# A two-block transformer on one core: sparse attention with the softmax's division on the output, and a schedule planned with other durations

## The chip, the cores and the metric

One Trainium2 chip, one core. The metric is the time of one execution on the device in microseconds (us); the median over runs is shown. The engines are PE (TensorE matmul; PEld is its weight load), DVE (VectorE), ACT (ScalarE), POOL (GpSimd) and SP (SyncE, which issues the DMAs).

## What is computed

Two layers of a hybrid attention model (latent attention, grouped attention, a depthwise convolution), then a second block with gated linear attention, a sparse attention, a feed-forward network and three layer norms, all over 1024 positions of width 1024. The part that the change rewrites is the sparse attention: 16 heads, 1024 queries, keys and values in one latent of 128, where a query sees the causal keys that an indexer selected (at most 256).

```python
def one_block(args):
    ...
    kv_sel = jax.vmap(lambda c, i: c[i])(ckv, idx)
    logits = jnp.einsum('bqhc,bqkc->bqhk', q_b, kv_sel).astype(jnp.float32) * (dc ** -0.5)
    logits = jnp.where(valid[:, :, None, :], logits, -jnp.inf)
    probs = jax.nn.softmax(logits, axis=-1).astype(kv_sel.dtype)
    return jnp.einsum('bqhk,bqkc->bqhc', probs, kv_sel)
...
o_b = dsa_attention(q_b, c_kv, iq_b, ik, iw_b)
o_b = jnp.einsum('blhc,hcd->blhd', o_b, w_uv[i]).reshape(B, L, DSA_HEADS * DSA_HEAD_DIM)
```

## The kernel before

The program is not written in the order in which it runs. Its text records operations (class `Plan`, calls such as `tt`, `act`, `copy`, `mm`, `tr`, `dma`): each has the tiles that it reads and writes, and in `alts` the engines that may run it with a price for each. Additions and subtractions between SBUF tiles may go to DVE or POOL, copies and casts to ACT or DVE, matmuls only to PE. `Plan.schedule` then plays through the program with these prices: whenever an engine is free in its model, it takes the ready operation that comes first in the text, within a window of 1500 operations. Where several engines could run an operation, it takes the cheapest, unless the wait there (its present work, and 0.6 us for each ready operation) is longer than the dearer price. The result is one fixed order per engine, and the assignment of operations to engines and tiles to slots: 89 pages of 128x512 (`pg`), 8 PSUM banks (`ps`), 8 small buffers (`sm`). On the chip every engine runs its list in order and waits by semaphores. The prices are written by hand, as `(n * 1.04 + 68) / 1000` us for an operation of n columns on DVE (`c_v`), `(n * 2.1 + 150) / 1000` on POOL (`c_p`), and likewise in `c_act`, `copy`, `scale`, `ts`, `mm` and `tr`.

Matrix products are made in three passes: each factor is split into a rounded part and the rest (`split`: a cast or copy and a subtraction), and three matmuls add up in PSUM. All of them are recorded by the same lines: L384 is `mm`, L388 `tr` (a transpose by PE), L325 and L327 are `tt` on DVE and on POOL, L284 is `act`, L293 a copy or cast on DVE, L335 `stt`, L347 `ts`, L358 and L360 `scale` on ACT and on DVE.

The sparse attention (tag `dsa`, from L1738) goes through 8 pairs of heads, 2 heads `i` in each and 2 halves `c` of the queries, 4 query blocks of 128 in each half: 32 units. A unit has three parts: *lead* (the scores of each block by matmuls, the mask's addition with the maximum at L1778, Exp with the sum, reciprocal at L1789, scaling of the probabilities), *loop* (per 128 keys the probabilities are transposed by PE, split and multiplied with the values into one PSUM accumulator), and an end that adds the two halves of the accumulator into `ob`. `pipeline` mixes each unit's lead into the loop of the unit before it. A half `c` = 0 sees one stretch of up to 512 keys (`nb` = 1), `c` = 1 two. Maximum, its scaled negative, sum and reciprocal are columns of a small buffer `sm`, one per query block.

Of the kernel before, what the change touches and what calls it, by code (L numbers as in the profile page):

```python
# [163 lines left out]
class Op:  # L164
    __slots__ = ("alts", "reads", "writes", "emit", "idx", "succ", "npred", "allocs", "table", "bufs", "tag", "pr", "late")
# [7 lines left out]
class Plan:  # L173
# [37 lines left out]
    def op(self, alts, reads, writes, emit, table=None):  # L211
        o = Op()
        o.alts = alts
        o.reads = [x for x in reads if isinstance(x, View)]
        o.writes = [x for x in writes if isinstance(x, View)]
        o.emit = emit
        o.table = table
        o.tag = self.tag
        o.late = self.late
        self.cur.append(o)  # L220
        return o
# [39 lines left out]
    def c_act(self, n, src, extra=0):  # L261
        return (n * 0.833 + (52 if isinstance(src, View) and src.psum else 93) + extra) / 1000
# [34 lines left out]
    def copy(self, out, in_, engs="av"):  # L297
        a = {}
        n = out.n
        if "v" in engs:  # L300
            a["v"] = (n * (1.04 if in_.psum else 0.52) + 68) / 1000
# [7 lines left out]
    def c_v(self, n, ex=0):  # L309
        return (n * 1.04 + 68 + ex) / 1000  # L310

    def c_p(self, n):
        return (n * 2.1 + 150) / 1000
# [26 lines left out]
    def ts(self, out, in0, s1, s2, op0, op1=None, accum=None):  # L340
# [8 lines left out]
        return self.op({"v": (out.n * (1.04 if in0.psum or accum is not None else 0.52) + 130 + (127 if accum is not None else 0)) / 1000},  # L349
                       [in0, s1, s2], [out, accum], emit)  # L350

    def scale(self, out, in_, col):
# [9 lines left out]
        return self.op({"v": (n * (1.04 if in_.psum else 0.52) + 130) / 1000, "a": self.c_act(n, in_, 93)},  # L362
# [17 lines left out]
    def mm(self, out, lhsT, rhs, start, stop, cost=None):  # L380
        n = rhs.n
        c = cost or max(n * 1.676 if rhs.ap.dtype == F32 or n < 256 else n * 0.4219, 60) / 1000
# [3 lines left out]
    def tr(self, out, in_, ident):  # L386
        return self.op({"t": 0.109}, [in_, ident], [out],
# [13 lines left out]
    def schedule(self, window=1500, dwindow=1200, boost=0, queue=0.25, verbose=False):  # L401
# [121 lines left out]
        while len(order) < N:  # L523
            progress = False
            for e in engs:
                while busy[e] <= now + 1e-9:
# [43 lines left out]
                    c = o.alts[e]  # L570
                    pre = None
# [797 lines left out]
BIG = -1.0e30  # L1369
# [65 lines left out]
def block2(N, X, Xd, ped, O, dbg=None):  # L1435
# [303 lines left out]
    for hp in range(8):  # L1739
        ob = {}  # L1740
# [18 lines left out]
        for i in range(2):  # L1759
# [5 lines left out]
            for c in C2:  # L1765
                pn = {}
                for t in range(4 * c, 4 * c + 4):
                    qs = slice((t % 4) * 128, (t % 4) * 128 + 128)
                    sm = P.buf("sm", (128, 4, 4), F32).rearrange("p a b -> p (a b)")
                    nb = 1 if t < 4 else 2  # L1770
                    for b in range(nb):
# [5 lines left out]
                        P.vec((n * 1.04 + 200) / 1000, [s, mk[t, b]], [p, sm[:, b:b + 1]],  # L1777
                              lambda e, p=p, s=s, n=n, m=mk[t, b], a=sm[:, b:b + 1]: nc.vector.tensor_tensor_reduce(  # L1778
                                  out=real(p), in0=real(s[:, 0:n]), in1=real(m), scale=1.0, scalar=BIG, op0=OP.add,
                                  op1=OP.max, accum_out=real(a)))  # L1780
                        pn[t, b] = p
                    if nb == 2:
                        P.tt(sm[:, 0:1], sm[:, 0:1], sm[:, 1:2], "max")
                    P.ts(sm[:, 2:3], sm[:, 0:1], -(128.0 ** -0.5), None, "mult")
                    for b in range(nb):
                        P.act(pn[t, b], pn[t, b], "Exp", bias=sm[:, 2:3], scale=128.0 ** -0.5, accum=sm[:, 4 + b:5 + b])
                    if nb == 2:
                        P.tt(sm[:, 4:5], sm[:, 4:5], sm[:, 5:6], "add")
                    P.vec(0.08, [sm], [sm], lambda e, sm=sm: nc.vector.reciprocal(real(sm[:, 6:7]), real(sm[:, 4:5])))  # L1789
                    for b in range(nb):  # L1790
                        P.scale(pn[t, b], pn[t, b], sm[:, 6:7])
# [22 lines left out]
                G, H = slice(64 * i, 64 * i + 64), slice(64 - 64 * i, 128 - 64 * i)  # L1814
                if i == 0:
                    ob[c] = P.pg()
# [3 lines left out]
                if i == 1:  # L1820
                    obd[hp, c] = P.dram((128, 512))
# [219 lines left out]
```

## Time and profile before

| | |
|---|---|
| median of 3 runs | 4151.16 us (4149.66 to 4156.11) |
| the profiled execution | 4150.0 us |
| its span | 4148.1 us |
| granted TensorE clock, mean | 0.98 |
| PE busy | 3908.4 us, 94% |
| DVE busy | 3306.3 us, 80% |
| ACT busy | 2036.4 us, 49% |
| POOL busy | 1430.2 us, 34% |

The busy time of an engine is the union of its instructions' spans. The slices of a page cut the span into 40 equal parts of some 104 us; each digit is the busy share in tenths. A wait's row names the engine and line that waited, and what released it. The granted clock is a share of 2.4 GHz; the records have two levels, 1.2 and 2.4 GHz.

### The profile page before, as it was taken

What the parts mean: (1) busy time and instruction counts of PE and PEld (TensorE: products, weight loads), DVE (VectorE), ACT (ScalarE), POOL (GpSimd) and SP (SyncE); (2) the same over time, 40 slices, a digit from 0 to 9 for tenths busy, and PEclk for the clock granted to TensorE, in tenths of its full rate; (3) what the DMA queues carried; (4) which work ended last, traced back from release to release, by engine and by line L of the source; (5) the groups of instructions that cost most, each with busy time, mean ns of one, the idle gap of its engine ahead of it and who ended that gap; (6) DMA issues with size and microseconds to landing.
All of it is one profiled execution on the core that took longest, in us unless ns stands there. A gap on an engine that the chain in (4) does not pass through costs nothing. (4 is left out here: it accounts for less than half of the span.)

```text
span 4148.1 us, 54250 instructions
## 1 busy us (share of the span) xinstructions
PE 3908.4 (94%) x18536; PEld 3153.5 (76%) x18536; DVE 3306.3 (80%) x5640; ACT 2036.4 (49%) x3969; POOL 1430.2 (34%) x1257
## 2 busy tenths in 40 slices
PE   7989998989989998999999999999999999999988
PEld 4768766667877776778878878888878788888867
DVE  8995899997896789985999996388886865455588
ACT  5244576774334566763545551366663432222245
POOL 4542455663142344552223441011132411121153
PEclk8999999999999999999999999999999999999998
DMA  7132211123323110042111142100044411111121
GB/s 254 62 117 72 62 54 53 50 70 114 110 83 99 39 34 26 16 133 94 67 44 54 67 142 77 62 31 30 32 144 152 137 51 49 49 41 46 56 82 57
DMA packets 184981, 311.88 MB, mean 75 GB/s; under 512 B 22912, under 2 KB 46208, under 8 KB 184704
## 3 DMA queue, kind: packets, MB, share of 16 engines
q1 hardware_dynamic: 184704, 308.42, 23.0%
q8 instruction: 146, 2.39, 0.2%
q14 instruction: 131, 1.07, 0.1%
HBM read 237.81 MB, written 62.39 MB: 72 GB/s over the span
## 5 line engine op out<-in xcount | busy, mean ns | idle before, releaser
L384 PE MATMUL ps<-pg,pg 128*128 128x512 f32 (+4 forms) x17200 | 3843.6, 380 | 119.1 <-ACT pg L284 43.5
L384 PEld LDWEIGHTS ps<-pg,pg 128*128 128x128 f32 (+2 forms) x17200 | 3009.0, 190 | 798.5 <-ACT pg L284 72.9
L327 POOL TENSOR_TENSOR pg<-pg,pg 128x512 fp32r<-128x512 f32 (+4 forms) x935 | 1355.7, 1462 | 2338.7 <-ACT pg L284 1301.7
L284 ACT ACTIVATE pg<-pg 128x512 fp32r<-128x512 f32 (+9 forms) x1529 | 875.5, 601 | 893.5 <-DVE pg L335 240.6
L325 DVE TENSOR_TENSOR pg<-pg,pg 128x512 fp32r<-128x512 f32 (+8 forms) x1126 | 956.2, 868 | 218.7 <-ACT pg L284 162.6
L284 ACT ACTIVATE pg<-ps 128x512 f32<-128x512 f32 (+9 forms) x1351 | 686.8, 557 | 801.4 <-PE ps L384 597.4
L325 DVE TENSOR_TENSOR pg<-ps,pg 128x128 fp32r<-128x128 f32 (+9 forms) x690 | 381.3, 567 | 209.2 <-PE ps L384 146.3
L335 DVE SCALAR_TENSOR_TENSOR pg<-ux,c,pg 128x512 f32<-128x512 f32 x416 | 348.7, 867 | 9.6 <-ACT pg L284 2.2
L368 DVE TENSOR_REDUCE sm<-ps 128x1 f32<-128x512 f32 (+1 forms) x492 | 326.1, 679 | 9.6 <-PE ps L384 7.0
L293 DVE CAST pg<-pg 128x512 fp32r<-128x512 f32 (+4 forms) x387 | 226.9, 596 | 72.0 <-ACT pg L284 34.0
L284 ACT ACTIVATE pg<-ps,c 128x512 f32<-128x512 f32 (+1 forms) x182 | 127.3, 708 | 250.0 <-PE ps L384 218.5
L335 DVE SCALAR_TENSOR_TENSOR pg<-pg,c,pg 128x512 f32<-128x512 f32 (+3 forms) x242 | 220.1, 946 | 5.5 <-ACT pg L284 5.2
L388 PE MATMUL ps<-c,pg 128*128 128x128 f32 (+1 forms) x796 | 180.2, 274 | 14.3 <-DVE pg L293 5.8
L293 DVE COPY ux<-ps 128x512 f32<-128x512 f32 x83 | 57.3, 690 | 143.3 <-ACT pg L284 133.6
L1523 DVE MAX8 sm<-ux 128x8 f32<-128x384 f32 (+5 forms) x192 | 168.8, 887 | 3.3
L1524 DVE MATCH_REPLACE8 ux<-sm,ux 128x384 f32<-128x384 f32 (+5 forms) x192 | 167.7, 875 | 0.0
L384 PE MATMUL ps<-pg,c 128*128 128x512 f32 (+3 forms) x196 | 85.2, 502 | 74.9 <-DVE pg L325 28.6
L388 PEld LDWEIGHTS ps<-c,pg 128*128 128x128 f32 (+1 forms) x796 | 107.6, 141 | 40.3 <-issue 6.2
L284 ACT ACTIVATE pg<-pg,sm 128x512 f32<-128x512 f32 (+2 forms) x192 | 116.2, 606 | 11.2 <-DVE sm L347 10.7
L384 PEld LDWEIGHTS ps<-pg,c 128*128 128x128 f32 (+2 forms) x196 | 33.6, 176 | 105.7 <-DVE pg L325 31.6
L671 ACT ACT_TABLE_LOAD x84 | 107.8, 1283 | 1.5
L1778 DVE CUSTOM_DVE_ANT_0 pg<-ps,pg 128x512 f32<-128x512 f32 (+3 forms) x176 | 100.0, 575 | 8.5 <-PE ps L384 6.3
(74 smaller groups left out, 1017.2 us busy)
## 6 DMA issues: line engine op xcount, KB each, us to landing
d<-pg SPq DMA_DIRECT2D x202, 256.0 KB, 2.1
pg<-d SPq DMA_DIRECT2D x178, 256.0 KB, 3.3
pg<-in_w2a SPq DMA_DIRECT2D x108, 256.0 KB, 2.8
pg<-in_wmod SPq DMA_DIRECT2D x96, 256.0 KB, 3.1
pg<-in_wup SPq DMA_DIRECT2D x88, 256.0 KB, 2.7
pg<-in_win SPq DMA_DIRECT2D x80, 256.0 KB, 3.3
pg<-in_wout SPq DMA_DIRECT2D x64, 256.0 KB, 3.3
pg<-in_wdn SPq DMA_DIRECT2D x48, 256.0 KB, 2.7
```

Of the source, the lines that this page charges most:

```text
L284: nc.scalar.activation(real(out), real(in_), fn, scale=real(scale), **k)
L293: self.nc.vector.tensor_copy(real(out), real(in_))
L325: self.nc.vector.tensor_tensor(out=real(out), in0=real(in0), in1=real(in1), op=o)
L327: self.nc.gpsimd.tensor_tensor(out=real(out), in0=real(in0), in1=real(in1), op=o)
L335: self.nc.vector.scalar_tensor_tensor(out=real(out), in0=real(in0), scalar=real(scalar), in1=real(in1), op0=o0, op1=o1)
L368: lambda e: self.nc.vector.tensor_reduce(out=real(out), in_=real(in_), axis=AX.X, op=o))
L384: lambda e: self.nc.tensor.matmul(real(out), lhsT=real(lhsT), rhs=real(rhs), start=start, stop=stop))
L388: lambda e: self.nc.tensor.transpose(real(out), real(in_), real(ident)))
L671: nc.scalar.preload_act_table_set(pre)
L1523: P.vec(P.c_v(n), [w], [m8], lambda e, m8=m8, w=w: nc.vector.max(real(m8), real(w)))
L1524: P.vec(P.c_v(n), [w, m8], [w], lambda e, m8=m8, w=w: nc.vector.match_replace(real(w), real(m8), real(w), MARK))
L1778: lambda e, p=p, s=s, n=n, m=mk[t, b], a=sm[:, b:b + 1]: nc.vector.tensor_tensor_reduce(out=real(p), in0=real(s[:, 0:n]), in1=real(m), sca ...
```

## The change

Three things are edited. In the sparse attention the four query blocks of a unit share one small buffer, so that the scaled negative maximum, the sum over the two stretches and the reciprocal are one operation on four columns each; the second stretch's maximum starts from the first's. The probabilities are not scaled any more: the four reciprocals are transposed by PE, spread over 64 partitions, into one PSUM bank, copied to `rr`, and the output `ob` of two heads is multiplied with it once. The prices are others, among them one for transposes that falls from 0.109 to 0.06 us. And an operation on DVE that reads SBUF alone (`dual`) gets dearer in the planner's model while POOL is busy there.

```diff
+        o.dual = "v" in alts and not any(x.psum for x in o.reads) and sum(x.n > 64 for x in o.reads) > 0
...
-        return (n * 0.833 + (52 if isinstance(src, View) and src.psum else 93) + extra) / 1000
+        return (n * 0.836 + (170 if isinstance(src, View) and src.psum else 202) + extra) / 1000
...
-            a["v"] = (n * (1.04 if in_.psum else 0.52) + 68) / 1000
+            a["v"] = (n * (1.04 if in_.psum else 0.52) + 155) / 1000
...
-        return (n * 1.04 + 68 + ex) / 1000
+        return (n * 1.04 + 155 + ex) / 1000
-        return (n * 2.1 + 150) / 1000
+        return (n * 2.2 + 200) / 1000
...
-        return self.op({"v": (out.n * (1.04 if in0.psum or accum is not None else 0.52) + 130 + (127 if accum is not None else 0)) / 1000},
+        return self.op({"v": (out.n * (1.04 if in0.psum or accum is not None else 0.52) + 190 + (127 if accum is not None else 0)) / 1000},
...
-        return self.op({"v": (n * (1.04 if in_.psum else 0.52) + 130) / 1000, "a": self.c_act(n, in_, 93)},
+        return self.op({"v": (n * (1.04 if in_.psum else 0.52) + 190) / 1000, "a": self.c_act(n, in_, 93)},
...
-        c = cost or max(n * 1.676 if rhs.ap.dtype == F32 or n < 256 else n * 0.4219, 60) / 1000
+        c = cost or max(n * 1.774 if rhs.ap.dtype == F32 or n < 256 else n * 0.4434 + 1, 60) / 1000
-        return self.op({"t": 0.109}, [in_, ident], [out],
+        return self.op({"t": 0.06}, [in_, ident], [out],
...
+                    if e == "v" and o.dual and busy["p"] > now:
+                        c += 0.42 * min(busy["p"] - now, c / 0.58)
```

(the planner's prices above; the sparse attention below)

```diff
@@ -1764,31 +1768,33 @@
                 split(*qq[c], o[c])
             for c in C2:
                 pn = {}
+                G, H = slice(64 * i, 64 * i + 64), slice(64 - 64 * i, 128 - 64 * i)
+
+                sm = P.buf("sm", (128, 4, 4), F32)
+                nb = 1 + c
                 for t in range(4 * c, 4 * c + 4):
                     qs = slice((t % 4) * 128, (t % 4) * 128 + 128)
-                    sm = P.buf("sm", (128, 4, 4), F32).rearrange("p a b -> p (a b)")
-                    nb = 1 if t < 4 else 2
+                    top = sm[:, 0, t % 4:t % 4 + 1]
                     for b in range(nb):
                         n = mw(t, b)
                         s = P.ps(max(n, 256))
                         N.mm(s, N.p3((qq[c][0][:, qs], qq[c][1][:, qs]),
                                      (cT[b][0][:, 0:max(n, 256)], cT[b][1][:, 0:max(n, 256)])))
                         p = P.pg()[:, 0:n]
-                        P.vec((n * 1.04 + 200) / 1000, [s, mk[t, b]], [p, sm[:, b:b + 1]],
-                              lambda e, p=p, s=s, n=n, m=mk[t, b], a=sm[:, b:b + 1]: nc.vector.tensor_tensor_reduce(
-                                  out=real(p), in0=real(s[:, 0:n]), in1=real(m), scale=1.0, scalar=BIG, op0=OP.add,
-                                  op1=OP.max, accum_out=real(a)))
+                        first = [top.k(t)] if b else []
+                        P.vec((n * 1.04 + 200) / 1000, [s, mk[t, b]] + first, [p, top.k(t)],
+                              lambda e, p=p, s=s, n=n, m=mk[t, b], a=top, b=b: nc.vector.tensor_tensor_reduce(
+                                  out=real(p), in0=real(s[:, 0:n]), in1=real(m), scale=1.0, scalar=real(a) if b else BIG,
+                                  op0=OP.add, op1=OP.max, accum_out=real(a)))
                         pn[t, b] = p
-                    if nb == 2:
-                        P.tt(sm[:, 0:1], sm[:, 0:1], sm[:, 1:2], "max")
-                    P.ts(sm[:, 2:3], sm[:, 0:1], -(128.0 ** -0.5), None, "mult")
+                P.ts(sm[:, 0, :], sm[:, 0, :], -(128.0 ** -0.5), None, "mult")
+                for t in range(4 * c, 4 * c + 4):
                     for b in range(nb):
-                        P.act(pn[t, b], pn[t, b], "Exp", bias=sm[:, 2:3], scale=128.0 ** -0.5, accum=sm[:, 4 + b:5 + b])
-                    if nb == 2:
-                        P.tt(sm[:, 4:5], sm[:, 4:5], sm[:, 5:6], "add")
-                    P.vec(0.08, [sm], [sm], lambda e, sm=sm: nc.vector.reciprocal(real(sm[:, 6:7]), real(sm[:, 4:5])))
-                    for b in range(nb):
-                        P.scale(pn[t, b], pn[t, b], sm[:, 6:7])
+                        P.act(pn[t, b], pn[t, b], "Exp", bias=sm[:, 0, t % 4:t % 4 + 1].k("e"), scale=128.0 ** -0.5,
+                              accum=sm[:, 1 + b, t % 4:t % 4 + 1].k((t, b)))
+                if nb == 2:
+                    P.tt(sm[:, 1, :], sm[:, 1, :], sm[:, 2, :], "add")
+                P.vec(0.2, [sm], [sm], lambda e, sm=sm: nc.vector.reciprocal(real(sm[:, 3, :]), real(sm[:, 1, :])))
                 lead = P.take(cut)
                 P.side()
                 acc = P.ps()
...
@@ -1811,13 +1817,18 @@
                         P.mm(d, st_, mv, j == 0 and z == 0, j == nj - 1 and z == 1)
                 loop = P.take(cut)
                 P.side()
-                G, H = slice(64 * i, 64 * i + 64), slice(64 - 64 * i, 128 - 64 * i)
+
+                rp = P.ps()
+                for t in range(4):
+                    P.tr(rp[0:64, t * 128:(t + 1) * 128], sm[:, 3, t:t + 1].to_broadcast([128, 64]), ident)
                 if i == 0:
-                    ob[c] = P.pg()
+                    ob[c], rr[c] = P.pg(), P.pg()
+                P.copy(rr[c][G, :].k(i), rp[0:64, :])
                 t = P.pg()
                 P.copy(t[G, :], acc[H, :])
                 P.tt(ob[c][G, :].k(i), acc[G, :], t[G, :], "add")
                 if i == 1:
+                    P.tt(ob[c], ob[c], rr[c], "mult", "vp")
                     obd[hp, c] = P.dram((128, 512))
                     P.dma(obd[hp, c], ob[c])
                 units.append([lead, loop, P.take(cut)])
```

The prices move instructions in the whole program. In total PE has 128 rows more, all of them transposes of `sm`; DVE has 5342 rows before and 4606 now, ACT 3747 and 3759 with every repetition counted, POOL 1262 and 1531. Three places:

POOL at the program's beginning, before. Subtractions `a<-b,c` are the rests of split weights; `pg_213` is a running sum of seven squares for the first norm.

```order
L327 TENSOR_TENSOR pg_136<-pg_94,pg_128 128x256
L327 TENSOR_TENSOR pg_158<-pg_104,pg_148 128x256
L327 TENSOR_TENSOR pg_213<-pg_213,pg_260 128x512
L327 TENSOR_TENSOR pg_314<-pg_221,pg_301 128x512
L327 TENSOR_TENSOR pg_333<-pg_227,pg_323 128x512
L327 TENSOR_TENSOR pg_365<-pg_249,pg_348 128x512
L327 TENSOR_TENSOR pg_385<-pg_262,pg_376 128x512
```

And now:

```order
L329 TENSOR_TENSOR pg_134<-pg_92,pg_122 128x512
L329 TENSOR_TENSOR pg_159<-pg_100,pg_138 128x256
L329 TENSOR_TENSOR pg_174<-pg_106,pg_154 128x256
L329 TENSOR_TENSOR pg_190<-pg_116,pg_171 128x256
L329 TENSOR_TENSOR pg_220<-pg_220,pg_227 128x512
L329 TENSOR_TENSOR pg_220<-pg_220,pg_249 128x512
L329 TENSOR_TENSOR pg_220<-pg_220,pg_266 128x512
```

POOL took one of the seven additions to the running sum before; now (`pg_220`) it takes four, three of them in a row, and the first split of a 128x512 weight.

PE in the first unit of the sparse attention, before: transposes of probabilities (L388, `c_82` is the identity, `ps_26610` and `ps_26621` are PSUM banks) among matmuls of the query projection (`ps_26495`, `ps_26597`).

```order
L388 MATMUL ps_26610<-c_82,pg_26529 128x128
L388 MATMUL ps_26621<-c_82,pg_26529 128x128
L384 MATMUL ps_26495<-pg_19133,pg_26322 128x512
L384 MATMUL ps_26597<-pg_19473,pg_26322 128x512
L384 MATMUL ps_26495<-pg_19145,pg_26322 128x512
L384 MATMUL ps_26597<-pg_19491,pg_26322 128x512
L384 MATMUL ps_26495<-pg_19133,pg_26329 128x512
L388 MATMUL ps_26610<-c_82,pg_26537 128x128
L388 MATMUL ps_26621<-c_82,pg_26537 128x128
L388 MATMUL ps_26610<-c_82,pg_26549 128x128
```

And now, at the end of that unit's transposes (`ps_26637` is the bank for the reciprocals, `sm_26532` their buffer):

```order
L390 MATMUL ps_26611<-c_82,pg_26549 128x128
L390 MATMUL ps_26617<-c_82,pg_26549 128x128
L390 MATMUL ps_26625<-c_82,pg_26549 128x128
L390 MATMUL ps_26635<-c_82,pg_26549 128x128
L390 MATMUL ps_26637<-c_82,sm_26532 64x128
L386 MATMUL ps_26505<-pg_19185,pg_26325 128x512
L390 MATMUL ps_26637<-c_82,sm_26532 64x128
L386 MATMUL ps_26505<-pg_19164,pg_26332 128x512
L390 MATMUL ps_26637<-c_82,sm_26532 64x128
L390 MATMUL ps_26647<-c_82,pg_26556 128x128
L390 MATMUL ps_26637<-c_82,sm_26532 64x128
L386 MATMUL ps_26505<-pg_19177,pg_26325 128x512
```

The four new transposes stand singly between projection matmuls and transposes of probabilities.

DVE inside the sparse attention, before: merges, scalings of the maximum and reciprocals of single query blocks, and a scaling of probabilities (L360).

```order
L1789 RECIPROCAL sm_28597<-sm_28597 128x1
L325 TENSOR_TENSOR sm_28622<-sm_28622 128x1
L325 TENSOR_TENSOR pg_28669<-ps_28644,pg_28669 128x4x64
L360 TENSOR_SCALAR pg_28613<-pg_28613,sm_28597 128x128
L347 TENSOR_SCALAR sm_28622<-sm_28622 128x1
L325 TENSOR_TENSOR sm_28658<-sm_28658 128x1
L325 TENSOR_TENSOR sm_28689<-sm_28689 128x1
L325 TENSOR_TENSOR pg_28727<-ps_28683,pg_28727 128x4x64
L347 TENSOR_SCALAR sm_28658<-sm_28658 128x1
L347 TENSOR_SCALAR sm_28689<-sm_28689 128x1
L325 TENSOR_TENSOR pg_28767<-pg_28681,pg_28754 128x512
```

And now, the same kinds of operation for one unit:

```order
L349 TENSOR_SCALAR sm_28472<-sm_28472 128x4
L327 TENSOR_TENSOR pg_28549<-ps_28519,pg_28549 128x4x64
L295 COPY pg_28612<-ps_28569 64x512
L327 TENSOR_TENSOR pg_28625<-ps_28569,pg_28612 64x512
L295 CAST pg_28642<-ps_28533 128x512
L327 TENSOR_TENSOR pg_28653<-ps_28533,pg_28642 128x512
L295 CAST pg_28662<-ps_28638 128x4x64
L295 CAST pg_28668<-ps_28614 128x512
L327 TENSOR_TENSOR sm_28472<-sm_28472 128x4
L327 TENSOR_TENSOR pg_28682<-ps_28614,pg_28668 128x512
L327 TENSOR_TENSOR pg_28691<-ps_28616,pg_28672 128x512
L1797 RECIPROCAL sm_28472<-sm_28472 128x4
```

One scaling, one merge and one reciprocal of 128x4 serve four blocks, and splits of probabilities (casts and subtractions) stand between them.

## Rows read from the trace of the kernel before

**Rows 1.** Page, parts 1 and 2: busy times; PE's and DVE's forty slices.

```profile
PE 3908.4 (94%) x18536; PEld 3153.5 (76%) x18536; DVE 3306.3 (80%) x5640; ACT 2036.4 (49%) x3969; POOL 1430.2 (34%) x1257
...
PE   7989998989989998999999999999999999999988
...
DVE  8995899997896789985999996388886865455588
```

**Rows 2.** Busy time by stretch: PE, PEld, DVE, ACT, POOL (instructions), granted clock, DMA.

```profile
0.00:300.00 300.00, 249.28 (x1151) 190.49 (x1152) 285.41 (x392) 128.15 (x236) 153.26 (x99) 0.93 0.44 146
...
500.00:900.00 400.00, 356.51 (x1584) 270.47 (x1584) 384.69 (x589) 283.24 (x551) 244.59 (x212) 0.96 0.17 50
...
1400.00:1800.00 400.00, 369.74 (x1579) 277.64 (x1578) 367.25 (x570) 268.56 (x497) 209.60 (x201) 0.98 0.12 35
...
2000.00:2500.00 500.00, 476.30 (x2634) 409.59 (x2633) 481.12 (x867) 266.56 (x572) 180.58 (x154) 0.99 0.23 79
...
2700.00:3000.00 300.00, 298.54 (x1658) 246.50 (x1657) 250.82 (x839) 201.75 (x517) 38.71 (x71) 1.00 0.10 31
...
3900.00:4100.00 200.00, 180.08 (x838) 147.18 (x837) 169.00 (x203) 88.92 (x145) 85.97 (x59) 0.95 0.21 63
...
4100.00:4148.00 48.00, 30.35 (x215) 28.70 (x214) 37.73 (x77) 24.78 (x53) 18.93 (x22) 0.80 0.21 68
```

**Rows 3.** Waits of PE in the whole span: total us, times, longest us.

```profile
PE ps L384 <- ACT pg L284: 52.5, 37, 8.7
PE ps L384 <- DVE pg L325: 47.0, 43, 8.2
...
PE ps L384 <- POOL pg L327: 28.7, 29, 5.9
```

**Rows 4.** Waits of PE from 2660 to 3090 us, the sparse attention.

```profile
PE ps L384 <- DVE pg L293: 2.0, 1, 2.0
PE ps L388 <- ACT pg L358: 1.6, 2, 1.3
PE ps L388 <- DVE pg L360: 1.4, 3, 0.8
```

**Rows 5.** Groups by line and form: operations of the sparse attention's softmax.

```profile
L284 ACT ACTIVATE pg<-pg,sm 128x512 f32<-128x512 f32 x96 | 68.4, 713 | 3.2 <-DVE sm L347 2.8
...
L284 ACT ACTIVATION_READ_ACCUMULATOR pg<-pg,sm 128x1 f32 x192 | 36.3, 189 | 0.0
...
L360 DVE TENSOR_SCALAR pg<-pg,sm 128x512 f32<-128x512 f32 x52 | 25.5, 492 | 1.0
...
L325 DVE TENSOR_TENSOR sm<-sm 128x1 f32<-128x1 f32 x128 | 25.0, 208 | 5.6 <-ACT pg L284 5.4
```

**Rows 6.** Timeline of PE in the sparse attention: start us, us, line, operation, count.

```profile
2864.05 0.27 PE L388 MATMUL ps<-c,pg 128*128 128x128 f32 x1
...
2866.03 0.60 PE L388 MATMUL ps<-c,pg 128*128 128x128 f32 x4
2866.38 4.83 PE L384 MATMUL ps<-pg,pg 128*128 128x512 f32 x20
```

**Rows 7.** Timeline of DVE and POOL: start us, us, line, operation, count.

```profile
702.00 1.82 DVE L325 TENSOR_TENSOR pg<-pg,pg 128x512 fp32r<-128x512 f32 x1
...
702.00 1.28 POOL L327 TENSOR_TENSOR pg<-pg,pg 128x512 fp32r<-128x512 f32 x1 [1.07 <-ACT pg L284]
...
2647.92 0.69 DVE L325 TENSOR_TENSOR pg<-pg,pg 128x512 fp32r<-128x512 f32 x1 [0.76 <-ACT pg L284]
...
3399.60 0.42 DVE L293 CAST pg<-pg 128x512 fp32r<-128x512 f32 x1
```

**Rows 8.** Groups by line and form, whole span: DVE and POOL on SBUF.

```profile
L327 POOL TENSOR_TENSOR pg<-pg,pg 128x512 fp32r<-128x512 f32 x714 | 1085.7, 1531 | 1659.3 <-ACT pg L284 830.4 <-DVE pg L293 358.5 <-PE ps L384 293.8
...
L325 DVE TENSOR_TENSOR pg<-pg,pg 128x512 fp32r<-128x512 f32 x555 | 487.3, 891 | 128.8 <-ACT pg L284 90.7 <-PE ps L384 22.8 <-POOL pg L327 7.0
...
L293 DVE CAST pg<-pg 128x512 fp32r<-128x512 f32 x297 | 184.2, 628 | 55.0 <-ACT pg L284 30.6 <-PE ps L384 18.6 <-DMA pg<-in_wout 3.5
```

More of the change, by code (lines that the diff above doesn't have):

```diff
@@ L164 @@
 class Op:
-    __slots__ = ("alts", "reads", "writes", "emit", "idx", "succ", "npred", "allocs", "table", "bufs", "tag", "pr", "late")
+    __slots__ = ("dual", "alts", "reads", "writes", "emit", "idx", "succ", "npred", "allocs", "table", "bufs", "tag", "pr", "late")
 BASIC = ("Copy", "Identity", "Square", "Abs", "Relu")
@@ L1739, in block2 @@
     for hp in range(8):
-        ob = {}
+        ob, rr = {}, {}
         cut = P.side()
```

## Prediction

> **What bounds the kernel now.** I began with the busy times and the forty slices [rows 1]: PE is busy for 94% of the span, DVE for 80%, and the slices show that the two are full in different places. So I cut the span where DVE's digit changes [rows 2]. In four stretches DVE is the fuller engine or close to it: 0 to 300 us (285.41 busy), 500 to 900 (384.69 of 400), 1400 to 1800 (367.25 of 400) and 2000 to 2500 (481.12 of 500). There PE is idle for 50.7, 43.5, 30.3 and 23.7 us, and its granted clock averages 0.93, 0.96, 0.98 and 0.99. From 2500 to 3900 PE's slices are nines: PE binds, and whatever DVE does is covered. The sparse attention, which the change rewrites, lies in this part (298.54 of 300 us on PE between 2700 and 3000, at a clock of 1.00, beside 250.82 on DVE). The last 250 us are a chain through all engines. PE's waits [rows 3] say the same: 52.5 us for ACT and 47.0 and 28.7 in the largest groups for DVE and POOL; in the sparse attention they are 5.0 us in all [rows 4].
>
> **Part 1: the softmax.** Per query block the maximum's merge, its scaling, the sum's merge, the reciprocal and the scaling of the probabilities go. On DVE 384 small operations become 80 of 128x4: 304 fewer at up to 208 ns [rows 5], some 50 us. The 192 scalings go, 96 each on DVE and ACT, 492 ns for each of the 52 largest on DVE [rows 5]. Added are 32 copies of 64x512, 16 products of 128x512 and 128 PE transposes of 64x128. All that DVE and ACT lose or gain here I cost at nothing: PE is the cover, and what the removed scalings made PE wait is 1.6 + 1.4 us [rows 4]. PE's addition has no cover. Four transposes back to back are busy for 0.60 us where one is for 0.27 [rows 6], so each further one takes 0.11: 128 x 0.11 = 14 us at most. The other end is -5, if the new ones fit into gaps and the 5.0 us of waits go. In the order 106 of the 128 stand singly between other matmuls, each a switch of its own; I take **+10**, near the dear end.
>
> Exp now waits for the scaled maxima of all four blocks, and the ACT queue behind it waits too. In the larger half, 7 Exps with their accumulator reads, 713 + 189 ns each [rows 5], lie between the last maximum and the first transposes: 6.3 us. I cost this at nothing because PE has the next head's query projection to put there, 48 matmuls of 512 columns at 4.83/20 = 0.24 us [rows 6], 11.6 us; the new order does mix the two. Without that cover each of 32 units loses up to 6 us. The new transposes wait for a reciprocal, as all transposes of probabilities did before. SP has 1402 rows before and after, in the planner's new order; each load is issued by the same step as before.
>
> **Part 2: the planner's durations.** The whole program is planned again. Counted over the new order, DVE loses 186 additions or subtractions of 128x512 and 33 of 128x256, POOL gains 202 and 33 (the 16 new products are in these counts), and some 60 casts go from DVE to ACT, which is busy for half of the span. Alone on SBUF, an add of 512 columns takes 0.69 us and a cast 0.42 [rows 7]; the 256-column add I put at half. DVE sheds 186 x 0.69 + 33 x 0.35 + 60 x 0.42 = 165 us.
>
> POOL takes 202 x 1.531 [rows 8] and 33 of half that, 334 us more, and DVE pays for it. At 702.00 an add on DVE lasts 1.82 us because a POOL operation of 1.28 began with it [rows 7]: it got through 0.54 us after POOL's end. The Trainium skill ("SBUF — State Buffer", section "Who interferes with whom") has this as a rule: a DVE instruction with two SBUF inputs and a POOL instruction that reads SBUF exclude each other, and the later is blocked for the whole of the other. The trace agrees at 702.00. Read alone, that rule speaks against moving additions to POOL; rival A gives its price. What DVE pays on the average is in the means: 891 - 690 for 555 adds and 628 - 420 for 297 casts [rows 8], 112 + 62 = 174 us, or 0.12 for each of POOL's 1430.2 us. That is the low end, two forms alone. If two thirds of DVE's 3306.3 us read SBUF alone (a guess) and pay the same 22%, it is 490 us, 0.34 for each POOL us: the high end. I take 0.28, nearer the high end as the other forms are many. 334 us then cost DVE 94 (40 to 114), and it sheds 71 net (51 to 125).
>
> How much of that is on the path? In the order DVE has 260 rows fewer ahead of the sparse attention, where it is full, and 94 fewer behind, where PE covers it: 260/354 of 71 is **-52 us**. If PE's gaps have another cause it is 0, the other end.
>
> The order can gain or lose by itself. The old plan priced the 512-column add at 0.600 us, the new one at 0.687 and more beside POOL, the trace has 0.891; for POOL it was 1.225 and is 1.326, against 1.531. Operands still come later than planned, but by less. PE idles for 148 us in the four stretches and 38 from 3900 on, and the clock withholds (1 - granted) x length, 21 + 16 + 8 + 5 + 10 + 10 = 70 us more [rows 2]. Half of these 256 is the most I grant (-128, with the 52 in it). The worst I put at POOL being waited for twice as long as in rows 3, with the lower clock behind it (+40). As the plan's error shrinks by about a third, I take a tenth of the 256, **-25**. In the last 48 us POOL's operations are 18.93/22 = 0.86 us and DVE's 0.49 [rows 2]; POOL gets some 8 more of the chain's last additions, **+3** (-2 to +8).
>
> Sum: -52 - 25 + 10 + 3 = -64. The profiled execution took 4150.0 us, its span of 4148.1 and 1.9 around it, and lies 1.2 under the median of 4151.16. 4150 - 64 = **4086 us**.
>
> **Rivals.** A: *the lock decides, slower.* The move to POOL turns to a loss where a POOL us costs DVE 165/334 = 0.49 us. At 0.6 DVE grows by 35 us, 26 of them on the path; with +10 and +3, and nothing from the order, 4189. For it: 702.00, and that DVE's two-input operations lie close in the full stretches, so each longer POOL stretch meets one. Against: the means give 0.12 to 0.34. Chance 0.13.
>
> B: *the relief doesn't reach PE*, since PE waits for ACT most (52.5 us) and for the order rather than for DVE. Then +10, +3 and an order term of -15 to +10 are left: 4148 to 4173. Against: DVE is 96% busy in two of the stretches and ACT 71% and 53%. Chance 0.15.
>
> C: *the truer plan closes half of PE's gaps*: -128 + 13, so 4035. For it: the clock rises with every gap that closes. Against: DVE can hardly be fuller than 96%. Chance 0.17.
>
> D: the division saves nothing because PE covers it; that is in the forecast.
>
> **Numbers.** The forecast has 0.55 and, with its terms' bounds, 4055 to 4125. The range of 4030 to 4165 takes in C's nearer half and most of B and leaves out A. About 0.2%, 8 us, is what a measurement of this kernel can tell from no change. Faster: forecast and C, 0.72. Same: 0.09 out of B. Slower: A and the rest of B, 0.19.
>
> **What would show it.** DVE's busy time falls by 100 to 150 us, 50 to 70 of it in the sparse attention; POOL's rises to about 1750. PE's idle time shrinks in the four stretches, and its clock there rises. The sparse attention stays full on PE and gets some 10 us longer. Wrong would be: DVE as busy as before ahead of 2500 us (A); DVE less busy there, but PE as idle (B); or PE waiting for Exp in the sparse attention, the cover that I counted on.

## The result, and the profile after

The changed kernel takes **4043.21 us** (median of 4 runs, 4038.25 to 4051.72) where the kernel before takes 4150.41 beside it: a ratio of 0.9742 (95% interval 0.9723 to 0.9762), 107 us less. The direction and the wide range hold. The size doesn't: 64 us were forecast, and 4043 lies below the 4055 to 4125 that the forecast's own terms allow. The profiled execution took 4043.23 us, its span is 4041.1.

The page of the changed kernel, busy times and four of the rows of slices, to be held against [rows 1]:

```profile
span 4041.1 us, 54342 instructions
PE 3885.0 (96%) x18664; PEld 3149.1 (78%) x18664; DVE 3187.4 (79%) x4915; ACT 2034.3 (50%) x3981; POOL 1778.2 (44%) x1526
PE   7999999999999999999999999999999999999996
DVE  8998898996797899976988996566775954456598
POOL 7654666774173565662244452111143611111177
PEclk8999999999999999999999999999999999999998
```

Span less busy time is PE's idle time: 4148.1 - 3908.4 = 239.7 us before, 4041.1 - 3885.0 = 156.1 now. So 83.6 us of the 107.0 by which the span shrinks are idle time, and 23.4 are PE's busy time, although 128 transposes came on top: the mean granted clock rose from 0.980 to 0.987, which over 4041 us is 28 us. It shows best in the part ahead of the sparse attention, where PE has the same 11681 rows in both kernels (before, then now; columns as in [rows 2]):

```profile
0.00:2669.00 2669.00, 2480.82 (x11681) 1981.56 (x11682) 2264.49 (x3530) 1401.56 (x2669) 1089.11 (x917) 0.98 0.25 80
...
0.00:2563.60 2563.60, 2450.50 (x11681) 1968.43 (x11682) 2207.16 (x3273) 1428.19 (x2742) 1326.12 (x1104) 0.99 0.25 83
```

The same rows take 30.3 us less there, and PE's idle time falls from 188.2 to 113.1 us. Over the whole program DVE lost 118.9 us, POOL gained 348.0.

The windows by stretch; everything behind the first lies up to 105 us earlier now, so the stretches are moved with the program (columns as in [rows 2]):

```profile
0.00:300.00 300.00, 263.18 (x1247) 203.10 (x1248) 284.00 (x346) 137.10 (x248) 186.20 (x127) 0.95 0.45 150
500.00:900.00 400.00, 370.78 (x1642) 278.73 (x1641) 378.81 (x556) 303.19 (x594) 283.56 (x239) 0.97 0.20 61
1300.00:1700.00 400.00, 383.59 (x1691) 294.97 (x1690) 362.32 (x562) 277.85 (x521) 239.55 (x225) 1.00 0.10 30
1900.00:2400.00 500.00, 498.03 (x2777) 432.03 (x2777) 450.67 (x815) 285.84 (x616) 207.36 (x190) 1.00 0.23 77
2600.00:2900.00 300.00, 300.00 (x1712) 247.63 (x1711) 210.28 (x565) 166.64 (x443) 46.63 (x74) 1.00 0.09 31
```

PE idles for 36.8, 29.2, 16.4 and 2.0 us in the four full stretches, where it was 50.7, 43.5, 30.3 and 23.7, and its clock reaches 1.00 in the last two. DVE is a little less full than in [rows 2] in all four, but only a little in the first three: 1.4, 5.9 and 4.9 us. PE is busy for about 14 us more in each of these, with an engine beside it that is nearly as busy as before. That by itself doesn't tell relief from order: an engine that others wait for can stay as full when work is taken off it, and simply get to its later work sooner.

The mask's addition with its maximum (L1786 now, L1778 before) shows where the sparse attention begins and ends:

```profile
L1778 DVE DVE_READ_ACCUMULATOR2_ANT sm<- x192: 72/83/86, 2669.0 to 3086.9; 128x1 f32 x192
...
L1786 DVE DVE_READ_ACCUMULATOR2_ANT sm<- x192: 72/83/86, 2563.6 to 2986.4; 128x1 f32 x192
```

It was 417.9 us long, and is 422.8 long: 5 us more, with PE full at clock 1.00 and without one wait. So all of the gain, 105 us, had come before it, and about 6 more come behind: from its end to the span's end 1061.2 us were needed before and 1054.7 now.

PE's waits over the whole span, against [rows 3]:

```profile
PE ps L386 <- POOL pg L329: 45.1, 53, 8.0
PE ps L386 <- DVE pg L327: 36.6, 22, 12.3
PE ps L386 <- ACT pg L286: 25.6, 25, 9.9
PE ps L386 <- DVE pg L295: 13.1, 17, 1.7
```

One large row of the kernel before, that for DVE's copies, belongs beside these:

```profile
PE ps L384 <- DVE pg L293: 43.8, 30, 5.7
```

The wait for ACT fell from 52.5 to 25.6 us, although ACT is as busy as before. The wait for POOL rose to 45.1, now the largest row. Added up by engine over all rows of the view, PE waited for DVE for 135.7 us before and 70.9 now, for ACT 57.4 and 26.5, for POOL 31.2 and 45.3: most of what PE gained are waits for DVE.

### The profile page after: what moved, and what is told of

Read it like the earlier page. It is cut to its first block, busy times and chain, and to the rows that moved or that the text cites. A ratio compares the mean times of both kernels' runs of the same rounds, so it can differ in the third digit from the quotient of the medians.

```text
span 4041.1 us, 54342 instructions
## 1 busy us (share of the span) xinstructions
PE 3885.0 (96%) x18664; PEld 3149.1 (78%) x18664; DVE 3187.4 (79%) x4915; ACT 2034.3 (50%) x3981; POOL 1778.2 (44%) x1526
## 5 line engine op out<-in xcount | busy, mean ns | idle before, releaser
L386 PEld LDWEIGHTS ps<-pg,pg 128*128 128x128 f32 (+3 forms) x17200 | 2991.1, 189 | 752.5 <-POOL pg L329 60.6
L329 POOL TENSOR_TENSOR pg<-pg,pg 128x512 fp32r<-128x512 f32 (+5 forms) x1188 | 1693.6, 1443 | 1882.9 <-ACT pg L286 999.4
L286 ACT ACTIVATE pg<-pg 128x512 fp32r<-128x512 f32 (+5 forms) x1605 | 910.4, 598 | 790.4 <-DVE pg L337 240.9
L286 ACT ACTIVATE pg<-ps 128x512 f32<-128x512 f32 (+12 forms) x1378 | 698.8, 552 | 893.9 <-PE ps L386 657.3
L327 DVE TENSOR_TENSOR pg<-pg,pg 128x512 fp32r<-128x512 f32 (+8 forms) x889 | 849.4, 969 | 134.7 <-ACT pg L286 91.9
L337 DVE SCALAR_TENSOR_TENSOR pg<-ux,c,pg 128x512 f32<-128x512 f32 x416 | 367.0, 909 | 22.5 <-ACT pg L286 15.3
L295 DVE CAST pg<-pg 128x512 fp32r<-128x512 f32 (+3 forms) x314 | 225.0, 724 | 43.6 <-ACT pg L286 21.0
L286 ACT ACTIVATE pg<-pg,sm 128x512 f32<-128x512 f32 (+1 forms) x192 | 115.6, 605 | 25.5 <-DVE sm L349 25.3
L295 DVE CAST pg<-ps 128x512 fp32r<-128x512 f32 (+5 forms) x108 | 55.8, 526 | 66.2 <-PE ps L390 26.8
```

The source lines that it names most:

```text
L286: nc.scalar.activation(real(out), real(in_), fn, scale=real(scale), **k)
L295: self.nc.vector.tensor_copy(real(out), real(in_))
L327: self.nc.vector.tensor_tensor(out=real(out), in0=real(in0), in1=real(in1), op=o)
L329: self.nc.gpsimd.tensor_tensor(out=real(out), in0=real(in0), in1=real(in1), op=o)
L337: self.nc.vector.scalar_tensor_tensor(out=real(out), in0=real(in0), scalar=real(scalar), in1=real(in1), op0=o0, op1=o1)
L386: lambda e: self.nc.tensor.matmul(real(out), lhsT=real(lhsT), rhs=real(rhs), start=start, stop=stop))
```

## The experiments

Theory 1, of the prediction's own sum: the relief of DVE carries the gain (52 of 64), the truer order adds some. Theory 2: the order carries it, and which engine does the work matters little. First the change was taken apart in four kernels, measured together, with the kernel before at 4151.61 us. (It took between 4150.4 and 4151.9 us beside all the runs below, so that their times can be held against each other.)

**Softmax alone, all old prices.** All prices of the diff at their old values, the rule for `dual` off.

> The softmax edit alone, planned with the old prices. By the prediction's part 1 (PE covers all that DVE and ACT lose in the sparse attention, and pays some 10 us for the new transposes): 4155 to 4165 us, DVE some 60 us less busy, all of it in the sparse attention. By its rival (DVE's and ACT's relief there does shorten the stage, so that part of the 107 us gained comes from the softmax): 4100 to 4140 us.

4158.91 us, 1.0018 (1.0009 to 1.0028): 7 us slower. Its page and PE's waits (`mm` is L395 in this kernel, copies L301, `tt` L333 and L335, `act` L292):

```profile
PE 3923.3 (94%) x18664; PEld 3163.7 (76%) x18664; DVE 3253.0 (78%) x5255; ACT 2006.4 (48%) x3910; POOL 1421.9 (34%) x1253
...
PE ps L395 <- DVE pg L333: 51.5, 47, 9.0
PE ps L395 <- ACT pg L292: 50.0, 34, 8.9
PE ps L395 <- DVE pg L301: 41.7, 31, 4.4
```

DVE does 53.3 us less, PE's waits are nearly those of before, and the time doesn't fall: what the softmax saves on DVE lies under PE. Whether the 7 us are what it adds to PE isn't shown, since two plans differ by about as much by accident (the placebo, below).

**The prices alone, old softmax.** The softmax's hunks taken back.

> The new prices alone, with the softmax as it was. If the whole gain is the planner's: 4030 to 4045 us, 0 to 10 under the changed kernel, which has the transposes on top. If the softmax has a share of the gain: 4070 to 4110 us.

4052.91 us, 0.9763 (0.9749 to 0.9778). The prices make the gain, although this is 8 us above the range expected for that. The changed kernel, with the new softmax, is 10 us faster still, which is hardly more than plans of the same kind differ by (the placebo, below).

**New order, old engines.** The program is recorded twice. The first plan, with old prices, only tells each operation's engine; the second, with new prices, sets the order and may not choose:

```diff
+    Q = record(tc, I, O, False)
+    Q.schedule(**OPTS)
+    on = {o.cid: e for _, e, o, _, _ in Q.order}
+    P = record(tc, I, O, True)
+    for o in P.cur:
+        o.alts = {on[o.cid]: o.alts[on[o.cid]]}
```

> The changed kernel with every operation held on the engine that a plan with the old prices gives it (POOL 1252 rows instead of 1526), and ordered with the new prices. If the gain is DVE's relief by POOL (my step): 4120 to 4160 us. If it is the truer order: 4045 to 4080 us, with DVE as busy as before and PE's idle time small all the same.

**Old order, new engines.** The same with `True` and `False` exchanged.

> The reverse: every operation on the engine that the new plan gives it, ordered with the old prices. If the gain is DVE's relief: 4050 to 4090 us. If it is the truer order: 4120 to 4160 us, though DVE is relieved.

The first took 4061.14 us, 0.9784 (0.9769 to 0.9799); the second 4170.12, 1.0043 (1.0028 to 1.0058), 10 us above the range of the truer order and far from that of the relief. The page and PE's waits of the new order on old engines:

```profile
PE 3903.0 (96%) x18664; PEld 3157.9 (78%) x18664; DVE 3225.0 (79%) x5255; ACT 1983.8 (49%) x3908; POOL 1411.5 (35%) x1253
...
PE ps L395 <- DVE pg L333: 40.2, 37, 11.3
PE ps L395 <- ACT pg L292: 33.1, 33, 8.6
PE ps L395 <- DVE pg L301: 21.8, 20, 3.4
PE ps L395 <- POOL pg L335: 12.8, 25, 1.9
```

and the page of the old order on new engines:

```profile
PE 3925.5 (94%) x18664; PEld 3166.7 (76%) x18664; DVE 3137.7 (75%) x4915; ACT 2038.5 (49%) x3981; POOL 1761.5 (42%) x1526
...
PE ps L395 <- DVE pg L301: 56.3, 36, 8.0
PE ps L395 <- ACT pg L292: 52.0, 30, 8.9
PE ps L395 <- DVE pg L333: 41.5, 36, 9.7
PE ps L395 <- POOL pg L335: 25.8, 24, 9.0
```

The four kernels with the new softmax, with PE's waits added up by engine over all rows:

| order, engines | time | DVE busy | PE waits for DVE | for ACT | for POOL |
|---|---|---|---|---|---|
| old, old | 4158.91 | 3253.0 | 137.0 | 53.2 | 28.5 |
| old, new | 4170.12 | 3137.7 | 141.1 | 52.2 | 26.1 |
| new, old | 4061.14 | 3225.0 | 95.1 | 33.3 | 12.8 |
| new, new (the change) | 4043.21 | 3187.4 | 70.9 | 26.5 | 45.3 |

This settles between the two theories. With the same operations on the same engines, the order alone is worth 4158.91 - 4061.14 = 98 us on the old engines and 4170.12 - 4043.21 = 127 on the new. In the old order the move to POOL takes 115 us off DVE, and PE waits for DVE as long as before; the kernel gets 11 us slower, hardly more than two plans differ by. On top of the new order the move is worth 4061 - 4043 = 18. DVE's busy time was not what PE waited for: PE waited for single results that the old plan had expected sooner. *Order* here is all that a plan sets besides the engines: the sequence on each queue and the slot of each tile. These two were not taken apart.

Then it was asked which price does it, and how far a plan scatters: four kernels more, with the kernel before at 4151.26 us.

**The rule for DVE beside POOL taken out.**

```diff
-                    if e == "v" and o.dual and busy["p"] > now:
-                        c += 0.42 * min(busy["p"] - now, c / 0.58)
```

> The changed kernel without the one rule that makes a DVE operation on SBUF alone dearer while POOL is busy; all the other new prices stay. Theory 1 (the order gains because the planner now believes that DVE's results come later, and most of that later comes from this rule): most of the 98 us are lost again, 4100 to 4150 us. Theory 2 (the fixed parts of the prices, 87 ns more for each operation of DVE and 110 to 120 for each of ACT, are enough): 4040 to 4065 us, with POOL's busy time about half way between 1422 and 1778, as 1372 rows stand on it where the changed kernel has 1526 and the old prices 1252.

4136.32 us, 0.9963 (0.9950 to 0.9976). Two lines carry 93 of the 107 us: theory 1. It isn't their effect on the engines: this kernel has 1373 rows on POOL and takes 4136, the one above with 1253 takes 4061.

```profile
PE 3916.4 (95%) x18664; PEld 3168.5 (77%) x18664; DVE 3254.2 (79%) x5175; ACT 1984.2 (48%) x3870; POOL 1576.0 (38%) x1373
...
PE ps L386 <- DVE pg L327: 68.2, 41, 8.9
PE ps L386 <- DVE pg L295: 44.5, 27, 6.0
PE ps L386 <- ACT pg L286: 27.2, 24, 10.2
PE ps L386 <- POOL pg L329: 16.8, 22, 1.9
```

Without the rule PE waits for DVE's two-input operations and copies for 68.2 + 44.5 = 112.7 us, with it for 36.6 + 13.1 = 49.7. The wait for ACT is as low as with the rule, and the other prices by themselves are worth 4159 - 4136 = 23 us. That it is ACT's price that lowers this wait isn't shown: the rule on old prices, below, has it at 31.3 us.

**Only PE's prices new.** All others old, the rule out.

> The new softmax, with only PE's prices new (a matmul of 512 columns 0.228 for 0.216 us, a transpose 0.06 for 0.109), all others old. If the gain of the order comes from the prices of DVE, ACT and POOL: 4150 to 4170 us, as with all prices old (4159). If PE's own prices carry it: 4060 to 4080 us. POOL has 1240 rows and stays at about 1410 us of busy time.

4218.37 us, 1.0159 (1.0144 to 1.0174): worse than either, which no line of the expectation had. My reading, argued and not tried further: slower matmuls beside a DVE that is as underpriced as ever make DVE's results look even earlier against PE than they are (2620 us planned on DVE beside 3678 on PE, where 2614 stood beside 3543).

**Only the other engines' prices new.** `mm` and `tr` at their old prices.

> The counterpart: the prices of DVE, ACT and POOL and the rule for DVE beside POOL are new, PE's are old. If these carry the gain: 4035 to 4060 us, PE idle for no more than some 160 us. If PE's prices carry it: above 4120 us. If both halves are needed: between, 4070 to 4120 us.

4041.71 us, 0.9734 (0.9719 to 0.9748): the whole gain.

**A placebo.** `n * 1.04 + 157` for 155 in `c_v`.

> The changed kernel with one price moved by 2 ns (157 for 155 in that of DVE's additions), which changes nothing that is true or false in the prices but gives another order: how far a new plan scatters by itself. If differences of 10 to 20 us between plans are accident: anything in 4030 to 4060 us. If the plan is steady: within 4 us of 4043.

4037.01 us, 0.9723 (0.9707 to 0.9739). Another order by 2 ns of a price is worth 6 us. PE's waits in it differ too, from 25.6 to 36.1 us for ACT and from 45.1 to 30.9 for POOL (the rows for `mm`). This is one draw and no bound; differences of up to some 10 us between two plans, and of some 15 us in one row of waits, are not read here as effects.

Four more, two in the same manner as before and two that try to go further (kernel before at 4151.93, for the last at 4150.84 us).

**The rule alone on old prices.**

> The new softmax and all old prices, with only the rule added that a DVE operation on SBUF alone takes longer while POOL is busy. Without the rule the changed kernel took 4136 us, with all old prices 4159. Theory 1 (the rule by itself carries the gain, the other prices little): 4050 to 4080 us. Theory 2 (the rule works only on prices that are near the measured durations): 4110 to 4150 us. By either, POOL with 1412 rows (1252 with all old prices) is busy for about 1600 us.

4084.35 us, 0.9843 (0.9826 to 0.9859): 75 us better than all old prices, between the two theories and nearer to the first (POOL 1631.2 us). The rule alone touches nothing but DVE's durations in the model, so most of the gain needs no other engine's price.

**The surcharge spread evenly.**

```diff
-                    if e == "v" and o.dual and busy["p"] > now:
-                        c += 0.42 * min(busy["p"] - now, c / 0.58)
+                    if e == "v" and o.dual:
+                        c += 0.00022 * o.reads[0].n
```

> The changed kernel with the rule's surcharge spread evenly: every DVE operation on SBUF alone takes 0.22 ns a column longer in the planner's model (0.11 us for 512 columns), whether POOL is busy or not; this adds up to what the rule adds in the changed kernel (283 us). Theory 1a (what counts is that DVE is planned as slow as it is): 4040 to 4065 us, as with the rule. Theory 1b (what counts is that the plan knows when, beside which POOL operation): 4100 to 4136 us, as without it. Theory 3 (what counts is that POOL gets more of the work): near 4070, as 1479 rows stand on POOL, between 1372 without the rule and 1526 with it.

4065.41 us, 0.9793 (0.9779 to 0.9808). Planning DVE as slow as it is on the average brings 71 of the rule's 93 us; 22 are left for knowing beside which POOL operation, more than the placebo's 6, but one draw against one draw. Theory 3 comes near this time too (4070), but the two kernels above with order and engines exchanged speak against it: 4061 us with 1253 rows on POOL, 4170 with 1526.

**The whole rest of POOL's operation as the surcharge.**

```diff
-                        c += 0.42 * min(busy["p"] - now, c / 0.58)
+                        c += busy["p"] - now
```

> The rule made as strong as the add beside a POOL operation in the trace of before shows it: in the model a DVE operation on SBUF alone takes longer by all that is left of POOL's operation, and not by 0.42 of the common time. The surcharges add up to 604 us where the changed kernel has 283; POOL has 1606 rows for 1526. If the order gains as the plan comes nearer to the chip: 4010 to 4035 us. If POOL, which PE already waits for most in the changed kernel (45.1 us), becomes the bound with 80 operations more: 4050 to 4090 us. If the plan is near enough already: 4033 to 4050.

4064.00 us, 0.9796 (0.9775 to 0.9817), in the range of the second theory and 21 us above the changed kernel. PE's wait for POOL rises from 45.1 to 60.8 us as that theory has it, but by little more than in the placebo's scatter, and its wait for ACT rises as well, from 25.6 to 45.0.

```profile
PE 3895.5 (96%) x18664; PEld 3163.2 (78%) x18664; DVE 3118.7 (77%) x4742; ACT 2071.7 (51%) x4068; POOL 1879.9 (46%) x1606
...
PE ps L386 <- POOL pg L329: 60.8, 83, 5.0
PE ps L386 <- ACT pg L286: 45.0, 38, 9.7
```

**POOL as slow as it is.**

```diff
+                    if e == "p":
+                        c *= 1.13
```

> The changed kernel with POOL's operations 13% longer in the planner's model, so that its prices add up to nearly what POOL takes on the chip: in the changed kernel's plan they add up to 1577 us where the trace has 1778, and PE waits for POOL most (45.1 us). If a plan gains whenever an engine's planned time comes nearer to its real time: 4015 to 4033 us, with PE's waits for POOL under 35 us. If DVE's was the only error that mattered: 4033 to 4053 us, the range of the last plans. If the model is now slow enough everywhere, and a dearer engine only moves the waits: 4053 to 4080. POOL has 1481 rows for 1526.

4033.66 us (5 runs, 4032.41 to 4036.72), 0.9722 (0.9707 to 0.9737). PE's wait for POOL falls to 32.8 us as expected, but it is 30.9 in the placebo, where POOL's price is as it was. The time is the lowest measured here and beats both kernels, but by 10 us against the changed one and 3 against the placebo, whose order is as good by luck. That POOL's price is an error that costs time isn't shown.

```profile
PE ps L386 <- DVE pg L327: 37.2, 27, 8.9
PE ps L386 <- POOL pg L329: 32.8, 35, 8.8
PE ps L386 <- ACT pg L286: 29.2, 24, 10.2
```

Side by side, what the planner's prices and surcharges for DVE add up to in each plan (summed by the kernel's own planner), and DVE's busy time on the chip:

| kernel | DVE in the plan | DVE on the chip | share | time |
|---|---|---|---|---|
| only PE's prices | 2620 | 3245 | 0.81 | 4218 |
| old order, new engines | 2448 | 3138 | 0.78 | 4170 |
| softmax, old prices | 2614 | 3253 | 0.80 | 4159 |
| before | 2660 | 3306 | 0.80 | 4151 |
| no rule | 2958 | 3254 | 0.91 | 4136 |
| rule alone | 2753 | 3209 | 0.86 | 4084 |
| flat surcharge | 3140 | 3185 | 0.99 | 4065 |
| new order, old engines | 3245 | 3225 | 1.01 | 4061 |
| prices, old softmax | 3167 | 3236 | 0.98 | 4053 |
| the change | 3103 | 3187 | 0.97 | 4043 |
| other engines' prices | 3117 | 3198 | 0.97 | 4042 |
| placebo | 3124 | 3183 | 0.98 | 4037 |
| POOL as slow | 3173 | 3184 | 1.00 | 4034 |
| whole wait | 3337 | 3119 | 1.07 | 4064 |

The plans fall into groups: with a share of 0.81 or less they take 4151 us and more, with 0.97 or more 4034 to 4065, and two lie between. Within the last group the share orders nothing: 0.99 takes 4065 us, 1.00 takes 4034 and 1.07 takes 4064, so that overshooting costs again isn't shown. The rule alone stands out: better at 0.86 than the kernel without it at 0.91. That it puts the delay where it occurs would explain it, and agrees with the 22 us above; no run takes that apart further. The other engines' prices are nearer to the chip in the changed plan as well, or beyond it (before and now: PE 0.90 and 0.95 of its busy time, POOL 0.81 and 0.89, ACT 0.89 and 1.10); what each of these is worth by itself was not measured, but for PE's.

## Why the prediction was right and wrong

- **The term that failed** is the split of the gain: "260/354 of 71 is -52" for the relief and "a tenth of the 256, -25" for the order. Measured: the order -98 or -127, the relief -18 with the new order and +11 without it. The 256 us of idle time and withheld clock were the right pot; the order took 38% to 50% of it and not a tenth. That 4043 lies in the stated range is owed to rival C, for whose sake the range went down to 4030, and not to the sum. "As the plan's error shrinks by about a third" was no way to size that: in the whole plan DVE's share went from 0.80 to 0.97, so five sixths of its error went. The prediction had looked at the add's price with nothing beside it (0.600 to 0.687, against 0.891) and left the rule for `dual`, the larger part, at "and more beside POOL".
- **The relief.** DVE's time did fall: 53 us by the softmax, and by the move a further 115 in the old order and 38 in the new, where 71 (51 to 125) had been worked out; in the changed kernel 57 us of the fall lie ahead of the sparse attention. An estimate from these: with the 165 us shed taken as right, DVE paid 50 and 127 us for the 340 and 367 that POOL gained, 0.15 and 0.35 for each, and the 0.28 that was taken lies between. (Its high end of 0.34 gave all forms the add's 22%; add and cast together lost 174 of some 680 us, 26%.) The step "how much of that is on the path" took DVE's fullness as a measure of the path. In the old order none of it was: rival B's "for the order rather than for DVE". Its other half, that PE waits for ACT most, was read from single rows; over all its rows DVE kept PE waiting for 135.7 us and ACT for 57.4.
- **Rival C** gave the time best: 4035 against 4043, for the reason that it named, and I gave it 0.17. Against it I put that DVE can hardly be fuller than 96%. It didn't have to get fuller. In the third stretch the new order on old engines has DVE as busy as in [rows 2] (368.83 us, where it was 367.25), and PE's idle time there is 16.6 us where it was 30.3:

```profile
1300.00:1700.00 400.00, 383.42 (x1694) 293.49 (x1694) 368.83 (x599) 265.27 (x500) 207.45 (x210) 1.00 0.11 32
```

- **Rival A, the lock.** DVE does pay for POOL's work, and the mean price was of the right size. The forms that answer to [rows 8]:

```profile
L329 POOL TENSOR_TENSOR pg<-pg,pg 128x512 fp32r<-128x512 f32 x864 | 1300.7, 1520 | 1426.6 <-ACT pg L286 772.9 <-PE ps L386 333.2 <-DVE pg L295 229.2
...
L327 DVE TENSOR_TENSOR pg<-pg,pg 128x512 fp32r<-128x512 f32 x405 | 407.0, 1014 | 83.4 <-ACT pg L286 53.1 <-PE ps L386 15.7 <-POOL pg L329 10.2
...
L295 DVE CAST pg<-pg 128x512 fp32r<-128x512 f32 x262 | 193.7, 747 | 32.0 <-ACT pg L286 21.0 <-PE ps L386 3.2 <-DMA pg<-in_wo 2.5
```

  The add went from 891 to 1014 ns and the cast from 628 to 747 as POOL went from 34% to 44%. (1014 - 690) x 405 + (747 - 420) x 262 is 217 us, 0.12 for each of POOL's 1778.2 us: the same low end as before, for the two forms. The Trainium skill ("SBUF — State Buffer", section "Who interferes with whom") says that a DVE instruction with two SBUF inputs and a POOL instruction that reads SBUF exclude each other. The trace agrees so far as the add, which has two such inputs, got slower beside more POOL work, 891 and then 1014 ns. Read as an argument against more POOL work the rule fails here on the new order, by 18 us, and on the old one the 11 us that it would explain are hardly above the scatter; read as a duration that a plan must know, it is the largest part of the gain. And the new order pays more of it: with the same operations on the same engines the add takes 932 ns in the old order and 1014 in the new, DVE is busy for 3137.7 and 3187.4 us, and still the new order is 127 us faster.
- **The softmax.** +10 was taken, bounds -5 and 14. Over the whole program it cost 7 us with the old prices (4 to 12 by the interval) and gained 10 with the new. Both are of the size of the scatter between plans, so the +10 is neither shown nor refuted; the sparse attention itself got 5 us longer. The cover held: PE waits for nothing in the sparse attention, neither for Exp nor for a reciprocal, where 5.0 us were lost in [rows 4].
- **The tail.** +3 was taken; the whole part behind the sparse attention got 6 us shorter. What of it is the last additions on POOL wasn't measured apart.
- **What would show it** came in: DVE down by 119, POOL at 1778, PE's gaps and clock in the four stretches better, the sparse attention full. None of these tells relief from order. The wait for ACT, which halved while ACT stayed as busy (2036.4 and 2034.3 us), is a hint: relieving DVE in the old order leaves it at 52.0 us. To tell them apart it took the kernels that change one and hold the other.

## What to carry to other kernels

Where a plan sets fixed queues, add up what it believes of each engine and hold that against the busy time on the chip: with DVE priced at 80% of its real time, and the others too low as well, the order cost 98 us here, without one instruction too many. Correct the durations relative to each other, the contended ones first (the rule for DVE beside POOL was worth 75 us by itself); one engine corrected alone (PE here, +59 us) can be worse than none. And before a plan's difference of 10 us is explained, run a placebo.

## What was not expected of the hardware

Beside more POOL work the mean of DVE's add rises and that of POOL's operation doesn't. The DVE add of 512 columns on SBUF takes 891, 1014 and 1056 ns where POOL is busy for 34%, 44% and 46% of the span; the POOL operation of that form 1531, 1520 and 1530. POOL isn't free of waiting for all that: at 702.00 its operation took 1.28 us [rows 7]. Nor does POOL's share alone set the add: in the old order on new engines it is 932 ns at 42%, where the flat surcharge has 999 at 42%. The third of each from the kernel with the whole wait, and the add of the old order:

```profile
L329 POOL TENSOR_TENSOR pg<-pg,pg 128x512 fp32r<-128x512 f32 x893 | 1350.0, 1530 | 1322.2 <-ACT pg L286 698.6 <-PE ps L386 231.6 <-DVE pg L295 183.8
L327 DVE TENSOR_TENSOR pg<-pg,pg 128x512 fp32r<-128x512 f32 x376 | 393.0, 1056 | 102.0 <-ACT pg L286 64.6 <-PE ps L386 17.2 <-POOL pg L329 12.0
...
L333 DVE TENSOR_TENSOR pg<-pg,pg 128x512 fp32r<-128x512 f32 x405 | 373.5, 932 | 144.2 <-ACT pg L292 113.1 <-POOL pg L335 12.3 <-PE ps L395 10.3
```

And where PE's gaps closed, its granted clock was higher: in the stretch whose idle time went from 30.3 to 16.4 us it went from 0.98 to 1.00, and in the one that went from 50.7 to 36.8 us from 0.93 to 0.95.
